# Sums of squares of four HGRN2 heads in quarters of the partitions, and first norm factors in the mixers' places, in a hybrid HGRN2 and Mamba-2 layer

## The chip, the cores and the metric

The kernel runs on one core of one Trainium2 chip. The metric is the device time of one execution in microseconds, and the number before the change is the median of three runs: 1939.81 us (1936.35 to 1941.0).

## The reference, cut to what matters

One layer on x of 2048 rows and 1024 columns. A projection of 6672 columns feeds 8 heads of an HGRN2 recurrence (128 keys, 128 values each) and 16 heads of Mamba-2 in two groups; both results are normed, concatenated to 2048 columns and projected back. The change touches the norm of each HGRN2 head, over its 128 values, and the place where its factor is applied:

```python
def hgrn2_mix(q_raw, f_raw, i_raw, g_raw, lb, norm_w):
    ...
    o = o.transpose(1, 0, 3, 2, 4).reshape(B_, L, HG_HEADS, HG_DV)
    o = o * lax.rsqrt(jnp.mean(o * o, axis=-1, keepdims=True) + EPS)
    o = o * norm_w.astype(jnp.float32).reshape(HG_HEADS, HG_DV)
    o = o.reshape(B_, L, HG_WIDTH) * jax.nn.silu(g_raw.astype(jnp.float32))
    return o.astype(q_raw.dtype)
def reference(x, norm_w, w_in, hg_lb_logits, hg_norm_w, m2_conv_w, m2_conv_b,
              m2_dt_bias, m2_a_log, m2_d_skip, m2_norm_w, w_out, final_norm_w):
    ...
        mix = jnp.concatenate([hg_out, m2_out], axis=-1)
        x = x + jnp.einsum('bse,ed->bsd', mix, w_out[l]).astype(x.dtype)
    return rmsnorm(x, final_norm_w)
```

## The kernel before, in words

**Tiling.** The 2048 rows are four blocks of TB = 512 (`tb`), each of NW = 4 windows of 128. Everything is kept transposed: features on the 128 partitions, rows along the free axis. A projection of 128 columns (`proj`, L344 to 354) is 24 matmuls of 128x512: weights and activations are each split into a high and a low part, and three products of 8 contraction steps are summed.

**Stages and their order.** The program is a list of jobs per block (`block_jobs`, L857 to 920): HGRN2 heads H(0) to H(7) (`hg_unit`, L608), four-part value projections VV (`v_step`), B and C of a Mamba-2 group (`bc_unit`), and eight units M of two Mamba-2 heads (`m2_unit`, L475). Each has projections, run one by one (`step`), and stages that are due a fixed count of projections later (`plan`, `flush`, L820 to 842). A head's stages m0 to m7 and mk are due 3 to 11 projections after its start (`DUES`), so the stages of neighbouring units stand between the projections of later ones. The Tile framework sets the semaphores; each engine works through its instructions in program order, and DMAs issued by SyncE (`nc.sync`) wait in SyncE's order too.

**The sums before.** Stage m6 of a head squares its output from PSUM into an "s" tile `on` (128x512) and stores the gated output to DRAM (`mix_d`). Stage m7 sums the squares over the partitions with `ss_cols` (L128): four matmuls, one per window, with the squares as weights and two columns of ones as the moving operand. VectorE copies the four column sums, GpSimd turns them into inverse roots with a power (`rstd_cols`, L120 to 123) in one column group of `nst`. At the block's end `rg_store` (L849) transposes `nst` (8 heads and 2 Mamba-2 groups, 40 rows) with TensorE, ScalarE copies it, and one DMA stores it to `rg_d[tb]`.

**Places in memory.** `slot` (L223) gives tiles of three tags in the mixers' pool `mp`: "s" (512 columns, 17 buffers), "b" (1024 columns, 8), "t3" (768, 2). The pool closes at `mid.close()` (L1018); pool `op` then uses its memory. Weights of the projection lie in `wp` with four buffers a tag (`wh`, `wl`, and three of `raw`) and are loaded PRE = 3 projections ahead (`w_get`, L112) through SyncE.

**Output projection** (L945 to 1071). Its blocks are the first three blocks and two halves of the last. `mix_get` (L961) loads a pair of normed-to-be rows e, e + 1 (`mr`), broadcasts their factors from `rg_d` to all partitions (`rgb`; for e < 8 one per head, L975), multiplies them in, and splits the result into `mh` and `ml`. `wo_get` (L947) loads one output weight and splits it (L952, L953). `out_mm` (L993) does three matmuls per output column group d. For block 0, five of eight column groups (`early`) of e = 0 to NE - 1 (NE = 8) are done in the last stages of the mixers, one `early_step` (L1010) a step; after `mid.close()` come e = NE to 15 for those five, then all 16 for the other three (`rest`). In the early steps the pairs e = 0 and 2 take the weights' `raw` buffers; the factors come from pool `o1`, with three buffers.

Of the kernel before, what the change touches and what calls it, by code (L numbers as in the profile page):

```python
# [7 lines left out]
F32 = mybir.dt.float32  # L8
# [30 lines left out]
def hybrid_layer(ctx, tc, xT, wt, wdt, wout, small, rows, out):  # L39
# [33 lines left out]
    rsk = rows[32:48].rearrange("(c h) -> h c", h=2)  # L73
    mhalf = cp.tile([P, 1], F32, name="mhalf")
    G.memset(mhalf, -0.5)
    epst = cp.tile([P, 1], F32, name="epst")
    G.memset(epst, EPS)

# [130 lines left out]
        V.tensor_add(sel, md32[0:32, 0:16], md32[0:32, 16:32])  # L209

    mix_d = [[dp.tile([P, TB], F32, name=f"mixd{e}_{t}") for t in range(NTB)] for e in range(16)]
    NR = (HG + 2) * NW
    rg_d = [dp.tile([NR, P], F32, name=f"rgd{t}") for t in range(NTB)]
    cs_d = [dp.tile([NW * M2H, P], F32, name=f"csd{t}") for t in range(NTB)]

    mid = ExitStack()
# [258 lines left out]
    def m2_unit(tb, g, c, ws, bcs, dts, sq, nst, r):  # L475
# [95 lines left out]
        def m3():  # L571
            ssv = ss_cols(sq["acc"], bank(f"mss{nm}"))
            ss = mp.tile([P, NW], F32, tag="mss", bufs=2, name=f"mss{nm}")
            V.tensor_copy(ss, ssv)
            rstd_cols(nst[:, HG + g, :], ss, 512)
        return [p0, p1], ([] if ct else [(1, ml)]) + list(zip(M0DUES if ct == 0 else MDUES, (md, m0, m1, m2))) + ([(9, m3)] if c == 3 else [])


# [26 lines left out]
                        A.copy(dst, ps)  # L605
        return [p0], []

    def hg_unit(tb, hd, ws, vrec, nst, r):  # L608
        nm = f"{hd}_{tb}"
        by32 = lambda a: a.rearrange("p (w t) -> p w t", t=32)  # L610

# [198 lines left out]
            advance(hgS[:, hd, :], NW - 1)  # L810

        def m7():
            ssv = ss_cols(r["on"], bank(f"hss{nm}"))
            ss = mp.tile([P, NW], F32, tag="hss", bufs=2, name=f"hss{nm}")
            V.tensor_copy(ss, ssv)
            rstd_cols(nst[:, hd, :], ss, P)
        return [pf, pq, pg], list(zip(DUES, (m0, m1, m2, m3, m4, mk, m5, m6, m7)))


# [28 lines left out]
    def rg_store(tb, nst):  # L848
        def m0():  # L849
            pt = bank(f"rgt{tb}")  # L850
            T.transpose(pt[0:NR, 0:P], nst.rearrange("p a w -> p (a w)"), ident)
            rgs = mp.tile([NR, P], F32, tag="cst", bufs=1, name=f"rgs{tb}")
            A.copy(rgs, pt[0:NR, 0:P])
            nc.sync.dma_start(rg_d[tb], rgs)
        return [], [(8, m0)]

    def block_jobs(tb):  # L857

        out_ = []
        dts, vrec, bcs, sq = {}, {}, {}, {}  # L860
        nst = mp.tile([P, HG + 2, NW], F32, tag="nst", bufs=2, name=f"nst{tb}")
        add = lambda fn, *args: out_.append((fn, args))

        def H(hd):
            add(hg_unit, tb, hd, [need(tb, c) for c in (8 + hd, hd, 24 + hd)], vrec.setdefault(hd // 4, {}), nst, {})

        def VV(q):
            ws = [need(tb, 16 + 4 * q + j) for j in range(4)]
            for j in range(4):
                add(v_step, tb, q, j, ws, vrec.setdefault(q, {}))  # L870

        def B(g):
            add(bc_unit, tb, g, [need(tb, 48 + g), need(tb, 50 + g)], bcs.setdefault(g, {}))

        def M(ct):
            add(m2_unit, tb, ct // 4, ct % 4, [need(tb, 40 + ct), need(tb, 32 + ct)], bcs.setdefault(ct // 4, {}),
                dts, sq.setdefault(ct // 4, {}), nst, {})

        def call(f):
            add(None, f)  # L880
        if tb == 0:
            H(0)
            VV(0)
            call(lambda: use(0))
        else:
            call(lambda: use(tb))
            VV(0)
        add(dt_unit, tb, dts)
        if tb:
            H(0)  # L890
        B(0)
        M(0)
        H(1)
        M(1)
        H(2)
        M(2)
        H(3)
        M(3)
        nxt = stats(tb + 1) if tb + 1 < NTB else [lambda: None] * 4
        call(nxt[0])  # L900
        VV(1)
        call(nxt[1])
        B(1)
        call(nxt[2])
        H(4)
        call(nxt[3])
        M(4)
        H(5)
        nxt = prep(tb + 1) if tb + 1 < NTB else [lambda: None] * 4
        M(5)  # L910
        call(nxt[0])
        H(6)
        call(nxt[1])
        M(6)
        call(nxt[2])
        H(7)
        call(nxt[3])
        M(7)
        add(rg_store, tb, nst)
        return out_  # L920
# [32 lines left out]
        V.tensor_sub(lo, raw, hi.bitcast(F32))  # L953
        wos[e] = (hi, lo)

    mixes, rgbs, xos = {}, {}, {}
    HB = TB // 2
    blocks = [(tb, 0, TB) for tb in range(NTB - 1)] + [(NTB - 1, 0, HB), (NTB - 1, HB, HB)]
    LAST = len(blocks) - 1
# [1 line left out]
    def mix_get(bl, e, lo=V):  # L961
# [8 lines left out]
            nc.sync.dma_start(mr[:, i, 0:n], mix_d[e + i][tb][:, cs_])  # L970
        if e < 8:
            for i in range(2):
                rgb = o1.tile([P, NW, P], F32, tag="rgb", bufs=3, name=f"rgh{bl}_{e}_{i}")[:, 0:n // P]
                r0 = (e + i) * NW + c0 // P
                nc.sync.dma_start(rgb, rg_d[tb][r0:r0 + n // P, :].partition_broadcast(P))  # L975
                V.tensor_tensor(mr[:, i, 0:n], mr[:, i, 0:n], rgb.rearrange("p w t -> p (w t)"), op=ALU.mult)
        else:
            if e in (8, 12):
                rgb = o1.tile([P, NW, P], F32, tag="rgb", bufs=3, name=f"rgb{bl}_{e}")[:, 0:n // P]
                r0 = (e // 4 + 6) * NW + c0 // P  # L980
                nc.sync.dma_start(rgb, rg_d[tb][r0:r0 + n // P, :].partition_broadcast(P))
                rgbs[bl, e // 4] = rgb.rearrange("p w t -> p (w t)")
# [20 lines left out]

    early = range(5)
    rest = range(5, KT)
    NE = 8
    o1 = ctx.enter_context(tc.tile_pool(name="o1", bufs=1))
    pss = {d: acc_bank(0, d) for d in early}

# [6 lines left out]
        step(lambda e=e: early_step(e))  # L1016
    flush(1 << 30)
    mid.close()  # L1018

    op = ctx.enter_context(tc.tile_pool(name="op", bufs=2))  # L1020
    accs, bks = {}, {}
# [110 lines left out]
```

## Time and profile before

| | |
|---|---|
| median of 3 runs (lowest, highest) | 1939.81 us (1936.35, 1941.0) |
| the profiled execution, its own time | 1938.97 us |
| its span in the trace | 1937.3 us |
| mean granted clock of TensorE | 0.990 |
| DVE (VectorE), share of the span | 62% |
| ACT (ScalarE), share of the span | 37% |
| POOL (GpSimd), share of the span | 17% |

PE is TensorE's matmuls, PEld its weight loads, which overlap them; SP is SyncE. Tile names stand without their numbers: `hss` is the sum of a head's squares, `on` the squares, `rgh` the factors of a pair e < 8, `woh` and `wol` the parts of an output weight, `po` the output projection's PSUM. A line such as L352 may be that of a helper that many stages call. In a timeline a row with a count is a run of like instructions, and its duration reaches from the first one's start to the last one's end. Matmuls are pipelined: one row's duration is longer than the distance to the next.

### The profile page before, as it was taken

Reading aid. Unit: us, or ns where it says so; the run is one execution under the profiler, and the core shown is the slowest. Engines: PE = TensorE matmul, PEld = TensorE weight load, DVE = VectorE, ACT = ScalarE, POOL = GpSimd, SP = SyncE. Lnnn points to the kernel's source line nnn. Section 1 sums busy time; section 2 is a strip of 40 time slices with the busy share of each in tenths; the row PEclk is TensorE's granted clock in tenths of the full one; section 3 lists DMA queues with packets and bytes.
Section 4 is the critical chain, followed back from the end, with each engine's and each line's share of the span. In section 5 each row is a group of like instructions: output and inputs, shape, how many; then the busy total and the mean of one; then the engine's idle time right before and its main releaser. Section 6 shows DMA issues by size and latency. Waiting matters only on the chain.

```text
span 1937.3 us, 34016 instructions
## 1 busy us (share of the span) xinstructions
PE 1895.2 (98%) x13418; PEld 1577.9 (81%) x13418; DVE 1203.2 (62%) x2920; ACT 710.3 (37%) x1170; POOL 323.2 (17%) x444
## 2 busy tenths in 40 slices
PE   7999999999999999999999999999999899999998
PEld 5788888788888888888888888888888777788897
DVE  8678768955565477547655874566366766534352
ACT  4446445533442353334333432334233433111111
POOL 4332242312011221110111211111101110000000
PEclk9999999999999999999999999999999899999998
DMA  8676876745555555455566554645455365524142
GB/s 267 246 261 240 285 256 227 267 153 176 178 172 195 177 194 185 150 172 180 163 207 189 194 173 143 194 156 167 169 186 164 133 240 177 201 82 152 47 134 88
DMA packets 118200, 355.44 MB, mean 183 GB/s; under 512 B 13032, under 2 KB 24472, under 8 KB 117656
## 3 DMA queue, kind: packets, MB, share of 16 engines
q1 hardware_dynamic: 116840, 352.00, 54.2%
q0 software_dynamic: 96, 0.03, 0.4%
q8 instruction: 106, 1.74, 0.4%
q10 hardware_dynamic: 1104, 1.24, 0.2%
q14 instruction: 54, 0.44, 0.1%
HBM read 273.30 MB, written 79.90 MB: 182 GB/s over the span
## 4 chain that ended last, share of the span: by engine, by line
PE 90%; DVE 5%; DMA 3%; ACT 1%; issue 1%; POOL 0%; ACTq 0%; DVEq 0%; SPq 0%; POOLq 0%
PE po L998 15%; PE px L352 9%; PE pz L352 9%; PE pf L352 9%; PE pv L597 9%; PE pq L352 9%; PE pg L352 8%; PE pB L352 2%; PE pC L352 2%; PE yd L546 2%; PE B L644 1%; PE o L804 1%; PE S L537 1%; PE hS L785 1%; PE o L803 1%; PE yo L557 1%
## 5 line engine op out<-in xcount | busy, mean ns | idle before, releaser
L998 PE MATMUL po<-mh,woh 128*128 128x512 f32 (+1 forms) x640 | 225.9, 355 | 9.7 <-ACT woh L952 9.7
L998 PE MATMUL po<-mh,wol 128*128 128x512 f32 (+1 forms) x640 | 224.3, 351 | 1.5 <-DVE wol L953 1.5
L998 PE MATMUL po<-ml,woh 128*128 128x512 f32 (+1 forms) x640 | 223.5, 351 | 2.0 <-DVE ml L989 2.0
L998 PEld LDWEIGHTS po<-mh,woh 128*128 128x128 f32 x640 | 122.3, 191 | 26.6 <-ACT woh L952 10.2
L998 PEld LDWEIGHTS po<-mh,wol 128*128 128x128 f32 x640 | 122.6, 192 | 19.3 <-DVE wol L953 3.4
L998 PEld LDWEIGHTS po<-ml,woh 128*128 128x128 f32 x640 | 122.1, 191 | 18.6 <-DVE ml L989 3.3
L988 ACT CAST mh<-mr 128x1024 fp32r<-128x1024 f32 (+1 forms) x48 | 43.4, 906 | 195.9 <-PE po L998 151.4
L989 DVE TENSOR_TENSOR ml<-mr,mh 128x1024 fp32r<-128x1024 f32 (+1 forms) x47 | 49.0, 1042 | 67.7 <-ACT mh L988 67.4
L510 DVE TENSOR_SCALAR csb<-csb,cs 128x128 f32<-128x128 f32 x256 | 66.7, 329 | 22.6 <-ACT ecs L507 22.6
L794 DVE SCALAR_TENSOR_TENSOR hSt<-hgS,totw,hS 128x128 f32<-128x128 f32 x32 | 11.0, 345 | 111.9 <-PE hS L785 99.2
L439 DVE SCALAR_TENSOR_TENSOR xs<-u_x,sm,xs 128x512 f32<-128x512 f32 x96 | 72.5, 755 | 4.2 <-ACT xs L437 3.7
L597 PE MATMUL pv<-wh,hh 128*128 128x512 f32 x224 | 72.0, 402 | 0.0
L569 POOL TENSOR_TENSOR sqa<-sqa,ecs 128x512 f32<-128x512 f32 x24 | 32.0, 1332 | 228.4 <-ACT ecs L568 191.9
L597 PE MATMUL pv<-wl,hh 128*128 128x512 f32 x224 | 69.5, 391 | 0.0
L597 PE MATMUL pv<-wh,hl 128*128 128x512 f32 x224 | 69.1, 390 | 0.0
L708 DVE TENSOR_TENSOR k<-k,tot 128x384 f32<-128x384 f32 x64 | 43.7, 683 | 40.8 <-PE B L644 40.8
L352 PE MATMUL px<-hh,wh 128*128 128x512 f32 x256 | 67.6, 406 | 0.0
L352 PE MATMUL pz<-hh,wh 128*128 128x512 f32 x256 | 67.6, 406 | 0.0
L352 PE MATMUL pq<-hh,wh 128*128 128x512 f32 x248 | 66.3, 410 | 0.0
L434 ACT COPY u_x<-px 128x512 f32<-128x512 f32 x32 | 18.8, 586 | 129.4 <-PE px L352 129.4
L352 PE MATMUL pf<-hh,wh 128*128 128x512 f32 x248 | 65.3, 405 | 0.0
L352 PE MATMUL pg<-hh,wh 128*128 128x512 f32 x248 | 65.0, 403 | 0.0
(333 smaller groups left out, 4597.8 us busy)
## 6 DMA issues: line engine op xcount, KB each, us to landing
wh<-whd SPq DMA_DIRECT2D x156, 512.0 KB, 4.3
wl<-wld SPq DMA_DIRECT2D x156, 512.0 KB, 3.4
whd<-wh SPq DMA_DIRECT2D x52, 512.0 KB, 3.4
wld<-wl SPq DMA_DIRECT2D x52, 512.0 KB, 3.0
wr<-wt SPq DMA_DIRECT2D x51, 512.0 KB, 5.3
csb<-csd SPq DMA_DIRECT2D x32, 512.0 KB, 5.5
mr<-mixd SPq DMA_DIRECT2D x64, 256.0 KB, 3.2
mixd<-sg SPq DMA_DIRECT2D x32, 256.0 KB, 2.0
```

Source lines behind the costliest of these rows:

```text
L352: state["mm"] = T.matmul(ps, lhsT=a[:, k, :], rhs=b[:, k, :], start=(n == 0), stop=(n == 23))
L439: V.scalar_tensor_tensor(dst, u[:, j:j + TB], cw[:, c, j:j + 1], dst, op0=ALU.mult, op1=ALU.add)
L510: V.tensor_scalar(csb[:, i, w, :], csb[:, i, w, :], dts["cs"][:, w, h0 + i:h0 + i + 1], 0.0, ALU.subtract, ALU.min)
L537: T.matmul(pS[:, sl], lhsT=bc["Bn"][:, w, :], rhs=xdc[:, sl], start=True, stop=True)
L546: T.matmul(pd[64 * i:64 * i + 64, w * P:(w + 1) * P], lhsT=xdt[:, w * P + i * 64:w * P + i * 64 + 64], rhs=csb[:, i, w, :], start=True, st ...
L557: T.matmul(po[:, sl], lhsT=prevs[w], rhs=bc["CT"][:, sl], start=True, stop=True)
L569: G.tensor_tensor(sq["acc"], sq["acc"], t, op=ALU.add)
L597: T.matmul(ps, lhsT=a[:, 2 * j + k, w * P:(w + 1) * P], rhs=rhs, start=(j == 0 and n == 0), stop=(j == 3 and n == 5))
L708: V.tensor_tensor(kv, kv, tt[:, :, 1:4].unsqueeze(3).broadcast_to([P, ng, 3, b]), op=ALU.mult)
L988: A.copy(mh[:, :, 0:n], mr[:, :, 0:n])
L989: lo.tensor_tensor(ml[:, :, 0:n], mr[:, :, 0:n], mh[:, :, 0:n].bitcast(F32), op=ALU.subtract)
L998: T.matmul(pss[d], lhsT=a[:, d, :], rhs=b, start=(e == 0 and n == 0), stop=(e == 15 and n == 2))
```

## The change

In m7 a head's squares go on a list `sqs` of its group of four heads, and nothing more is done until the fourth (heads 3 and 7). Then four matmuls with 32 columns of 1/128 as weights (`mean32`) and the four heads' squares as moving operands give the means of squares, each in its own 32 partitions of one PSUM tile. ScalarE copies the tile into the place of the fourth head's squares; SyncE stores one row of each quarter to `rg_d` (16 rows of 128), loads these 2048 values as 128 x 16, GpSimd takes mean + EPS to the power -1/2, and SyncE stores them back. `nst` and `rg_store` keep the two Mamba-2 groups only.

In the output projection's early steps the factors for e = 0 and 2 (four tiles) are taken from the "s" places while the mixers' pool is open; the `rgb` tag of `o1` has two buffers instead of three. NE is 9: one more early step, with seven output weights in `o1` and seven in `op`.

```diff
@@ -73,6 +73,8 @@
     rsk = rows[32:48].rearrange("(c h) -> h c", h=2)
     mhalf = cp.tile([P, 1], F32, name="mhalf")
     G.memset(mhalf, -0.5)
+    mean32 = cp.tile([P, 32], F32, name="mean32")
+    G.memset(mean32, 1.0 / P)
     epst = cp.tile([P, 1], F32, name="epst")
     G.memset(epst, EPS)
 
@@ -209,8 +211,8 @@
         V.tensor_add(sel, md32[0:32, 0:16], md32[0:32, 16:32])
 
     mix_d = [[dp.tile([P, TB], F32, name=f"mixd{e}_{t}") for t in range(NTB)] for e in range(16)]
-    NR = (HG + 2) * NW
-    rg_d = [dp.tile([NR, P], F32, name=f"rgd{t}") for t in range(NTB)]
+    NR = 2 * NW
+    rg_d = [dp.tile([(HG + 2) * NW, P], F32, name=f"rgd{t}") for t in range(NTB)]
     cs_d = [dp.tile([NW * M2H, P], F32, name=f"csd{t}") for t in range(NTB)]
 
     mid = ExitStack()
@@ -572,7 +574,7 @@
             ssv = ss_cols(sq["acc"], bank(f"mss{nm}"))
             ss = mp.tile([P, NW], F32, tag="mss", bufs=2, name=f"mss{nm}")
             V.tensor_copy(ss, ssv)
-            rstd_cols(nst[:, HG + g, :], ss, 512)
+            rstd_cols(nst[:, g, :], ss, 512)
         return [p0, p1], ([] if ct else [(1, ml)]) + list(zip(M0DUES if ct == 0 else MDUES, (md, m0, m1, m2))) + ([(9, m3)] if c == 3 else [])
 
 
@@ -605,7 +607,7 @@
                         A.copy(dst, ps)
         return [p0], []
 
-    def hg_unit(tb, hd, ws, vrec, nst, r):
+    def hg_unit(tb, hd, ws, vrec, sqs, r):
         nm = f"{hd}_{tb}"
         by32 = lambda a: a.rearrange("p (w t) -> p w t", t=32)
 
@@ -810,10 +812,22 @@
             advance(hgS[:, hd, :], NW - 1)
 
         def m7():
-            ssv = ss_cols(r["on"], bank(f"hss{nm}"))
-            ss = mp.tile([P, NW], F32, tag="hss", bufs=2, name=f"hss{nm}")
-            V.tensor_copy(ss, ssv)
-            rstd_cols(nst[:, hd, :], ss, P)
+
+            sqs.append(r["on"])
+            if len(sqs) < 4:
+                return
+            ps = bank(f"hss{nm}")
+            for j in range(4):
+                T.matmul(ps[32 * j:32 * j + 32, :], lhsT=mean32, rhs=sqs[j], start=True, stop=True)
+            rr = sqs[3]
+            A.copy(rr, ps)
+            flat = rg_d[tb][(hd - 3) * NW:(hd + 1) * NW, :].rearrange("w t -> (w t)")
+            nc.sync.dma_start(flat.rearrange("(j t) -> j t", j=4), rr.rearrange("(j r) t -> j r t", r=32)[:, 0, :])
+            rc = mp.tile([P, 16], F32, tag="rc", bufs=2, name=f"rc{nm}")
+            fold = flat.rearrange("(p c) -> p c", c=16)
+            nc.sync.dma_start(rc, fold)
+            rstd_cols(rc, rc, 1)
+            nc.sync.dma_start(fold, rc)
         return [pf, pq, pg], list(zip(DUES, (m0, m1, m2, m3, m4, mk, m5, m6, m7)))
 
 
@@ -851,18 +865,18 @@
             T.transpose(pt[0:NR, 0:P], nst.rearrange("p a w -> p (a w)"), ident)
             rgs = mp.tile([NR, P], F32, tag="cst", bufs=1, name=f"rgs{tb}")
             A.copy(rgs, pt[0:NR, 0:P])
-            nc.sync.dma_start(rg_d[tb], rgs)
+            nc.sync.dma_start(rg_d[tb][HG * NW:(HG + 2) * NW, :], rgs)
         return [], [(8, m0)]
 
     def block_jobs(tb):
 
         out_ = []
-        dts, vrec, bcs, sq = {}, {}, {}, {}
-        nst = mp.tile([P, HG + 2, NW], F32, tag="nst", bufs=2, name=f"nst{tb}")
+        dts, vrec, bcs, sq, hsq = {}, {}, {}, {}, {}
+        nst = mp.tile([P, 2, NW], F32, tag="nst", bufs=2, name=f"nst{tb}")
         add = lambda fn, *args: out_.append((fn, args))
 
         def H(hd):
-            add(hg_unit, tb, hd, [need(tb, c) for c in (8 + hd, hd, 24 + hd)], vrec.setdefault(hd // 4, {}), nst, {})
+            add(hg_unit, tb, hd, [need(tb, c) for c in (8 + hd, hd, 24 + hd)], vrec.setdefault(hd // 4, {}), hsq.setdefault(hd // 4, []), {})
 
         def VV(q):
             ws = [need(tb, 16 + 4 * q + j) for j in range(4)]
@@ -953,7 +967,7 @@
         V.tensor_sub(lo, raw, hi.bitcast(F32))
         wos[e] = (hi, lo)
 
-    mixes, rgbs, xos = {}, {}, {}
+    mixes, rgbs, xos, mixer_done = {}, {}, {}, []
     HB = TB // 2
     blocks = [(tb, 0, TB) for tb in range(NTB - 1)] + [(NTB - 1, 0, HB), (NTB - 1, HB, HB)]
     LAST = len(blocks) - 1
@@ -970,13 +984,15 @@
             nc.sync.dma_start(mr[:, i, 0:n], mix_d[e + i][tb][:, cs_])
         if e < 8:
             for i in range(2):
-                rgb = o1.tile([P, NW, P], F32, tag="rgb", bufs=3, name=f"rgh{bl}_{e}_{i}")[:, 0:n // P]
+                nm = f"rgh{bl}_{e}_{i}"
+                rgb = slot("s", [NW, P], nm) if e < 4 and not mixer_done else o1.tile(
+                    [P, NW, P], F32, tag="rgb", bufs=2, name=nm)[:, 0:n // P]
                 r0 = (e + i) * NW + c0 // P
                 nc.sync.dma_start(rgb, rg_d[tb][r0:r0 + n // P, :].partition_broadcast(P))
                 V.tensor_tensor(mr[:, i, 0:n], mr[:, i, 0:n], rgb.rearrange("p w t -> p (w t)"), op=ALU.mult)
         else:
             if e in (8, 12):
-                rgb = o1.tile([P, NW, P], F32, tag="rgb", bufs=3, name=f"rgb{bl}_{e}")[:, 0:n // P]
+                rgb = o1.tile([P, NW, P], F32, tag="rgb", bufs=2, name=f"rgb{bl}_{e}")[:, 0:n // P]
                 r0 = (e // 4 + 6) * NW + c0 // P
                 nc.sync.dma_start(rgb, rg_d[tb][r0:r0 + n // P, :].partition_broadcast(P))
                 rgbs[bl, e // 4] = rgb.rearrange("p w t -> p (w t)")
@@ -1003,7 +1019,7 @@
 
     early = range(5)
     rest = range(5, KT)
-    NE = 8
+    NE = 9
     o1 = ctx.enter_context(tc.tile_pool(name="o1", bufs=1))
     pss = {d: acc_bank(0, d) for d in early}
 
@@ -1016,6 +1032,7 @@
         step(lambda e=e: early_step(e))
     flush(1 << 30)
     mid.close()
+    mixer_done.append(True)
 
     op = ctx.enter_context(tc.tile_pool(name="op", bufs=2))
     accs, bks = {}, {}
```

## Rows read from the trace of the kernel before

**Rows 1.** The page's chain that ended last: its shares by engine.
```profile
PE 90%; DVE 5%; DMA 3%; ACT 1%; issue 1%; POOL 0%; ACTq 0%; DVEq 0%; SPq 0%; POOLq 0%
```

**Rows 2.** Windows: start:end, us, busy (count) of each engine, PE clock, DMA, GB/s.
```profile
60.00:1526.00 1466.00, 1463.01 (x11026) 1211.76 (x11025) 936.65 (x2486) 586.14 (x992) 278.77 (x398) 1.00 0.58 191
345.00:385.00 40.00, 37.01 (x304) 30.77 (x303) 36.59 (x78) 19.27 (x33) 14.16 (x14) 0.96 0.77 283
1531.00:1549.00 18.00, 10.97 (x78) 8.66 (x77) 15.72 (x32) 9.60 (x12) 4.18 (x5) 0.72 0.77 258
1580.00:1601.00 21.00, 16.96 (x61) 12.68 (x59) 9.76 (x10) 7.23 (x8) 1.54 (x1) 0.84 0.60 223
```

**Rows 3.** PE's waits: for what, us in total, times, longest.
```profile
PE po L998 <- ACT woh L952: 9.7, 2, 6.0
```

**Rows 4.** Timeline of PE around two sums: start, duration, line, operation.
```profile
1502.60 0.95 PE L129 MATMUL hss<-ones,on 128*128 128x2 f32 x8
1503.47 0.33 PE L738 MATMUL H<-qa,k 128*32 128x32 f32 x16
...
1507.49 1.98 PE L352 MATMUL pq<-hl,wh 128*128 128x512 f32 x8
1509.40 0.45 PE L760 MATMUL G<-qa,k 128*64 128x64 f32 x8
...
1573.95 0.39 PE L998 MATMUL po<-ml,woh 128*128 128x512 f32 x1
1574.18 0.95 PE L129 MATMUL hss<-ones,on 128*128 128x2 f32 x8
1574.98 0.49 PE L998 MATMUL po<-mh,woh 128*128 128x512 f32 x1
1575.31 0.40 PE L998 MATMUL po<-mh,wol 128*128 128x512 f32 x1
```

**Rows 5.** PE: timeline at hb and B; line 149 (min/median/max ns); group of B.
```profile
324.74 1.02 PE L149 MATMUL hb<-dg_h,ones 128*128 128x512 f32 x2
...
L149 PE MATMUL hb<-dg_h,ones x6: 591/592/595, 324.7 to 1086.9; 128*128 128x512 f32 x6
...
1525.26 0.55 PE L644 MATMUL B<-MB,k 128*32 128x48 f32 x32
1525.74 0.50 PE L352 MATMUL pz<-hh,wh 128*128 128x512 f32 x1
...
L644 PE MATMUL B<-MB,k 128*32 128x48 f32 x2048 | 35.4, 210 | 3.9 <-DVE MB L681 3.9
```

**Rows 6.** Line 123: count, ns min/median/max, first to last start, form.
```profile
L123 POOL TENSOR_TENSOR rsx<-rsx,mhalf x4: 1008/1025/1852, 28.4 to 1033.8; 128x4 f32<-128x4 f32 x4
L123 POOL TENSOR_TENSOR orz<-orz,mhalf x1: 697/697/697, 1927.7 to 1927.7; 128x2 f32<-128x2 f32 x1
```

**Rows 7.** DMA issues: queue, count, KB each, median us to landing.
```profile
csd<-cst SPq DMA_DIRECT2D x4, 32.0 KB, 2.1
...
rgh<-rgd SPq DMA_DIRECT2D x32, 256.0 KB, 3.6
```

**Rows 8.** Timeline of SyncE's queue: start, us to issue, line, transfer.
```profile
1502.79 0.32 SPq L102 DMA_DIRECT2D wh<-whd  x1
...
1531.53 1.27 SPq L975 DMA_DIRECT2D rgh<-rgd  x3
```

**Rows 9.** Timeline at qa, dg_h, xdc; line 699 with its first and last start.
```profile
1084.95 0.28 ACT L699 COPY qa<-MB 128x128 f32<-128x128 f32 x1
1085.06 1.03 DVE L148 TENSOR_SCALAR dg_h<-ident,rsx 128x128 f32<-128x128 f32 x4
...
L699 ACT COPY qa<-MB x32: 283/289/300, 45.9 to 1533.8; 128x128 f32<-128x128 f32 x32
...
1555.12 0.69 DVE L523 TENSOR_TENSOR xdc<-xn,dec 128x512 f32<-128x512 f32 x1 [0.19 <-ACT xn L521]
```

**Rows 10.** The chain that ended last, 1580 to 1600 us, in order.
```profile
1584.14 1.31 DMA rgd<-rgs
```

## The prediction, made before the changed kernel ran

> **What bounds the kernel now.** I read the page's chain first: TensorE is 90% of the work that ended last [rows 1], VectorE the next with 5%. The windows then say where this is true. From 60 to 1526 us PE is busy 1463.01 of 1466 us at the granted clock 1.00, so there each microsecond of PE work is a microsecond of time [rows 2]. Three other stretches lose time [rows 2]. From 345 to 385, the end of the first block, PE is busy 37.01 of 40 us and VectorE, on which it then waits, 36.59. From 1531 to 1549, where the output projection begins, PE is busy 10.97 of 18 us at a granted clock of 0.72; by the waits of PE its longest one there (6.0) is for the first output weight's cast [rows 3]. From 1580 to 1601, where the mixers' memory is given back, it is busy 16.96 of 21 us at 0.84, and the other of the two waits in rows 3 (9.7 in all) stands there. The profiled execution took 1938.97 us, 1.67 more than its span and 0.84 less than the median of the runs; the sum is made against 1938.97. A measurement of this kernel tells about 0.3%, 5.8 us, from no change.
>
> **Sums removed.** Each of 32 heads has four matmuls with two moving columns, eight passes [rows 4]. The passes are short, but each loads 128 columns of weights first. Before wide matmuls: from the last wide start at 1573.95 to the second after the sums, 1575.31, is 1.36 us; two steps of a stream take 0.46 (eight wide passes take 1.98, the last alone 0.39, so one step is 0.23). The sums cost 0.90 [rows 4]. Before a group that uses quarters of the array: they hold PE from 1502.60 to 1503.47, 0.87. Without them such a group starts 0.32 after the last wide start (1509.40 against 1507.49 + 1.98 - 0.39 = 1509.08), 0.09 over a step, so they cost 0.78 [rows 4]. The first head of the kernel and every fourth one stand before wide work, nine in all: 9 x 0.90 + 23 x 0.78 = 26.0 us.
>
> **Sums added.** Eight times, four matmuls of 32 weight columns over 512 columns of f32, two passes each. The nearest pass of this length and type is the broadcast of the row factors: two take 1.02, one 0.59, so a step is 0.43 [rows 5]. Whether four go beside each other is read from the group B: 32 passes of 48 columns into the four quarters. One after another they would take 32 x 0.43 x 48/512 = 1.29; they take 0.55 less the last one's 0.21, 0.34, nearly a quarter [rows 5]. So two steps, 0.86. Changing shape costs 0.09 going in and 0.10 coming out (the next wide start is 0.14 after B's last, which streams 0.04), and the second wide start comes 0.33 instead of 0.23 later [rows 4, 5]. That is 1.15 each, 9.2 in all. Bounds: 6.9 without changes of shape; 8 x (8 x 0.43 + 0.29) = 29.8 if none overlap. I take 9.2, since B has the same shape and only fewer columns. Net -16.8.
>
> The Trainium skill, "TensorE: Matmul & The Clock Gate", section "Measured speedup vs the span model", gives less for 512 columns: 3.07 times for four row tiles, 2.38 for three column tiles. By 3.07 the two steps would be 1.12 and the whole result 2 us later; no run here shows it yet, and B's rows speak for nearly four.
>
> **Off the path.** VectorE loses 32 copies of four columns, ScalarE gains eight copies of 512 columns (128 take 0.28 [rows 9], so between that and 1.1; I take 0.6), and the transposition of the factors shrinks from 40 to 8 rows: nothing, as PE work hides them. GpSimd's power on 16 columns isn't in the trace: two columns take 0.70, four 1.02 [rows 6], so 0.16 a column gives 2.9 us; bounds 1.0 and 4.1. SyncE issues three small transfers in a row for each four heads: store, load, store, each waiting for what the one before it brings. A small store lands in 2.1, a broadcast load in 3.6 [rows 7], so the chain is 0.6 + 2.1 + (2.1 to 3.6) + 3.1 + 2.1, 10 to 11.5 us. GpSimd stands in it too, with the convolutions' products and the att copies behind it. On SyncE the next weights and csb loads stand behind it; the weights of the last pz were asked for at 1502.79 and used at 1525.74 [rows 5, 8], 23 us ahead, about 18 after landing. So a chain is hidden seven times of eight, up to a length of 18 us; beyond it, every microsecond counts. The last one isn't hidden (below).
>
> **First block.** By its end PE would come some 3.6 us earlier (a quarter of 16.8, less what is still to come), but VectorE gives back only eight short copies and is full. I take 3 us of the 16.8 as lost there, between 0 and 5.
>
> **First norm factors.** Before, SyncE stood still for the projection memory and asked for the first three factor loads together at 1531.53 [rows 8], when the last projection had ended. The edit puts the four of e = 0 and 2 in "s" slots, but places with one tag seem to be handed out in program order: the broadcast dg_h needs only rsx, whose last power began at 1033.8 [rows 6], yet it was written at 1085.06, just after the "s" tile that precedes it in the program, qa at 1084.95 [rows 9]. The last "s" tile ahead of the first factors is qa of the last head, written at 1533.81, later than 1531.53. So they are asked for about 2.3 us later, behind the loads for e = 4 and 6, which still go into the freed memory: a loss of 1 to 5, I take 2.5. The factors of e = 2 stand in the program behind the last xdc, which was written at 1555.12 [rows 9], about when PE came to e = 2; if its place is older than that the load costs nothing, else some 6, I take 2. Together +4.5. If the order does not bind, the loads land before 1531 and the 7.03 us in which PE idles from 1531 to 1549 go, and a share of 10.97 us at lowered clock, some 10 in all, of which VectorE (15.72 busy of 18 [rows 2]) lets about 8 through.
>
> **One more early step, and the give-back.** The mixers' memory now waits for the last chain instead of the factor store, which landed at 1584.14 + 1.31 = 1585.45 [rows 10], 11.3 after the last head's sums began at 1574.18 [rows 4]. The new chain ends 11 to 12.6 after them. But PE has 15 more matmuls, 3.45 us, before it needs that memory. What then ends last is the weight load that needs the freed memory for its cast, shifted alike. So 3.45 less 0 to 1.3: -2, with bounds -6 and +2.
>
> **Two buffers for factors instead of three.** In the second pass over block 0 each pair would wait for a load (3.6) and two products (0.69 each, as xdc in rows 9), 5.0 us, where PE uses a pair in 18 x 0.23 = 4.1; only four pairs come so and mixes run up to four ahead. +1, between 0 and 4. The later blocks use a pair in 11 us, or 5.7 with half the columns: nothing.
>
> **Sum:** -16.8 + 3 + 4.5 - 2 + 1 = -10.3, so 1928.7.
>
> **The rivals.**
> Early factors (0.17): the places are free and the loads go ahead, so the gap at 1531 closes. For it: SyncE had nothing else to do for 28 us; against it: the order in rows 9. The place then gives -8 instead of +4.5: 1916.
> Sums one after another (0.10, slower): at 512 columns the four streams do not overlap, or a head's second pass holds back the next head's first. Place: PE, eight times; price 29.8 instead of 9.2. It decides from 3.0 us a group on, where the removal is used up. Then +3.8 + 4.5 - 2 + 1, and no lead for the first block to take: 1946. Against it stands B.
> Held squares (0.13): three more of 17 "s" slots are held for up to a hundred microseconds, so a drain of PSUM takes a slot just read and waits for a lagging engine; with two projection banks PE feels it once the wait passes a projection (24 wide steps, 5.5 us). At 0.3 us a head 10 us go: 1938. Against it: nothing yet waits so in steady state.
> Chains too long (0.10): SyncE or GpSimd stand longer than 18 us in some of the eight chains; 4 us each for four of them: 1944. Against it: the landings.
>
> **How the numbers follow.** The forecast has 0.50, 1928.7; its own range is 1921 to 1936. To hold 8 in 10 the range reaches down through the early factors and up through held squares to the lower part of the slow cases: 1912 to 1944. Faster by over 0.3%: 0.47 of the forecast, all 0.17, 0.04 of the others, 0.68. Within: 0.20, most of it held squares and chains. Slower: 0.12, from the serial sums and long chains.
>
> **What would show it.** Eight groups hss of 8 passes, about 1.1 us of PE each (1 right, 3.7 serial); windows from 60 to 340 and 400 to 1500 shorter by 2 and 10 us with PE full; PE waits near 345 to 385 longer than 3 us; the factor loads of e = 0 after 1533 in the old time, and the first wait of the output projection 6 to 9 us; at the give-back a wait for a cast of e = 9 under 3.6. PE waiting for a weight or for an "s" tile in the middle of a block would make the sum wrong, as would factor loads well ahead of the last projection.

## The result, and the profile after

The changed kernel takes 1922.87 us (median of 4 runs, 1920.79 to 1926.49), the kernel before 1939.46 in the same comparison; the ratio is 0.9918 (95% interval 0.9899 to 0.9938). That is 16.6 us less where 10.3 were forecast: inside the range, and larger than forecast. The profiled execution took 1923.20 us with a span of 1921.3, so the pair of profiles differs by 15.8 us.

The windows of the changed kernel, columns as in [rows 2]; the four stretches are the ones shown of before, moved with the work:

```profile
60.00:1512.00 1452.00, 1448.25 (x10845) 1182.95 (x10844) 934.68 (x2460) 589.81 (x1000) 262.07 (x354) 1.00 0.58 194
345.00:385.00 40.00, 36.25 (x296) 29.63 (x295) 37.08 (x76) 19.57 (x33) 14.53 (x12) 0.96 0.80 291
1517.00:1535.00 18.00, 9.83 (x90) 7.59 (x88) 14.88 (x31) 8.47 (x12) 3.63 (x5) 0.72 0.68 222
1566.00:1587.00 21.00, 19.20 (x88) 15.10 (x87) 8.76 (x10) 5.49 (x7) 7.31 (x6) 1.00 0.58 213
```

TensorE is as full and at full clock in the blocks as before, only shorter. The start of the output projection is no better (9.83 us busy of 18 at a granted clock of 0.72, against 10.97 [rows 2]); the give-back is much better (19.20 of 21 at 1.00, against 16.96 at 0.84).

The timeline of PE in the changed kernel: the last projection, the first matmul of the output projection, that of its third step (e = 2), and the last group of sums:

```profile
1511.83 0.50 PE L354 MATMUL pz<-hh,wh 128*128 128x512 f32 x1
...
1528.75 0.79 PE L1014 MATMUL po<-mh,woh 128*128 128x512 f32 x1 [8.01 <-ACT woh L966]
...
1547.76 0.50 PE L1014 MATMUL po<-mh,woh 128*128 128x512 f32 x1 [0.53 <-ACT mh L1004]
...
1563.98 0.39 PE L1014 MATMUL po<-ml,woh 128*128 128x512 f32 x1
1564.30 1.07 PE L821 MATMUL hss<-on,mean 128*32 128x512 f32 x8
1565.29 0.50 PE L1014 MATMUL po<-mh,woh 128*128 128x512 f32 x1
1565.63 0.39 PE L1014 MATMUL po<-mh,wol 128*128 128x512 f32 x1
```

and the groups of the two new operations, the sums and GpSimd's power on 16 columns:

```profile
L821 PE MATMUL hss<-on,mean 128*32 128x512 f32 x64 | 8.5, 605 | 0.0
...
L125 POOL TENSOR_TENSOR rc<-rc,mhalf 128x16 f32<-128x16 f32 x8 | 23.3, 2912 | 0.7
```

The sums cost TensorE what was worked out: from the wide start at 1563.98 to the second one after them, 1565.63, are 1.65 us, less two steps of 0.23 leaves 1.19 (forecast 1.15). Eight passes of 605 ns lie in 1.07 us.

To see where the time went, the starts of the same matmul are compared: the first head of the second block (`pf`), the last projection (`pz`), and then, counted from the last projection, the first matmul of the output projection, that of its third and of its eighth step; the way from the eighth step to the twelfth, with the give-back in it; from there to block 1; the first 96 matmuls of block 1; and the rest to the end. All are read from the timelines of PE, one profile each (the experiments' labels are told below):

| kernel | 2nd block | last pz | first | 3rd step | 8th step | give-back | to block 1 | block 1 | rest |
|---|---|---|---|---|---|---|---|---|---|
| before | 435.87 | 1525.74 | 14.96 | 28.48 | 53.60 | 20.92 | 51.25 | 24.71 | 261.05 |
| changed | 433.68 | 1511.83 | 16.92 | 35.93 | 58.13 | 16.02 | 50.51 | 22.63 | 262.13 |
| e1 sums only | 431.76 | 1509.93 | 14.96 | 27.17 | 55.10 | 22.02 | 51.44 | 23.05 | 261.18 |
| e2 places only | 437.92 | 1527.78 | 17.17 | 37.57 | 59.75 | 19.67 | 51.31 | 24.19 | 261.34 |
| e3 nine steps only | 439.19 | 1529.12 | 14.96 | 29.01 | 56.90 | 16.13 | 51.29 | 22.67 | 261.03 |
| e4 no places | 434.24 | 1512.39 | 14.96 | 26.94 | 53.43 | 15.68 | 51.59 | 22.63 | 261.77 |
| e5 early request | 434.24 | 1512.41 | 8.83 | 17.15 | 43.70 | 18.51 | 50.24 | 23.68 | 261.11 |
| e6 ACT's queue | 435.95 | 1514.12 | 17.75 | 39.05 | 63.24 | 16.07 | 50.53 | 22.63 | 261.15 |
| e7 = e4, small tiles outside | 435.23 | 1512.66 | 14.96 | 27.24 | 53.67 | 13.88 | 51.31 | 23.21 | 261.06 |
| e8 = e1, small tiles outside | 432.82 | 1510.25 | 14.97 | 27.28 | 55.29 | 13.90 | 51.51 | 23.71 | 262.02 |
| e9 = e5, small tiles outside | 431.15 | 1508.59 | 8.84 | 17.16 | 45.22 | 15.46 | 49.89 | 22.63 | 261.06 |
| e10 serial sums | 435.65 | 1529.14 | 16.92 | 37.15 | 62.98 | 15.15 | 51.07 | 22.63 | 261.66 |
| e11 sums twice | 433.95 | 1517.46 | 17.51 | 37.06 | 61.22 | 15.46 | 50.91 | 22.63 | 261.14 |
| e12 early request only | 440.25 | 1530.09 | 8.84 | 18.04 | 44.92 | 20.15 | 51.03 | 23.67 | 261.06 |

Of the 16.0 us between the two spans, 13.9 are there by the last projection. The tail then loses 4.5 up to the eighth step and wins 4.9 at the give-back, 0.7 before block 1 and 2.1 at its start; the end takes 1.1 back. The chain that ended last shows the two places, the first factors and the give-back (start, duration, work):

```profile
1519.14 0.24 PE o L806 x2
1519.43 5.25 DMA rgh<-rgd
1524.70 1.27 DVE mr L992
...
1565.35 2.41 POOL ml L1005
1567.77 2.52 DMA mr<-mixd
...
1572.96 2.90 POOL rc L125
1575.88 0.32 SPq L830
...
1576.30 1.22 DMA rgd<-rgs
...
1577.84 1.05 ACT woh L966
1578.89 0.04 issue
1578.94 21.08 PE po L1014 x91
```

The first two rows: the load of the first factors could only start (1519.43) when the matmuls `o` of the last head but one had read the place it was given (1519.14 + 0.24). The last rows: GpSimd's power, the store of the factors, behind it in SyncE's queue the store of the Mamba-2 rows (1576.30), and only when that has landed the casts into freed memory.

### The profile page after: what moved, and what is told of

The parts are those of the page before. It is cut to its first block, busy times and chain, and to the rows that moved or that the text cites. A ratio compares the mean times of both kernels' runs of the same rounds, so it can differ in the third digit from the quotient of the medians.

```text
span 1921.3 us, 33571 instructions
## 1 busy us (share of the span) xinstructions
PE 1877.7 (98%) x13226; PEld 1546.0 (80%) x13226; DVE 1197.7 (62%) x2887; ACT 713.3 (37%) x1178; POOL 306.2 (16%) x398
## 4 chain that ended last, share of the span: by engine, by line
PE 92%; DVE 4%; DMA 2%; issue 1%; ACT 1%; POOL 0%; DVEq 0%; ACTq 0%; SPq 0%; POOLq 0%
PE po L1014 18%; PE px L354 9%; PE pz L354 9%; PE pf L354 9%; PE pv L599 9%; PE pq L354 9%; PE pg L354 8%; PE pB L354 2%; PE pC L354 2%; PE yd L548 2%; PE B L646 2%; PE o L806 1%; PE o L805 1%; PE S L539 1%; PE yo L559 1%; PE hS L787 1%
## 5 line engine op out<-in xcount | busy, mean ns | idle before, releaser
L1014 PE MATMUL po<-mh,woh 128*128 128x512 f32 (+1 forms) x640 | 223.0, 352 | 10.3 <-ACT woh L966 9.8
L1014 PEld LDWEIGHTS po<-mh,woh 128*128 128x128 f32 x640 | 121.5, 190 | 28.2 <-ACT woh L966 10.3
L1014 PEld LDWEIGHTS po<-mh,wol 128*128 128x128 f32 x640 | 121.6, 190 | 16.8 <-DVE wol L967 1.1
L438 POOL COPY hist<-u_x 128x3 f32<-128x3 f32 x32 | 9.7, 304 | 395.7 <-ACT u_x L436 395.6
L436 ACT COPY u_x<-px 128x512 f32<-128x512 f32 x32 | 18.8, 587 | 128.7 <-PE px L354 128.7
```

Source lines behind the costliest of these rows:

```text
L1014: T.matmul(pss[d], lhsT=a[:, d, :], rhs=b, start=(e == 0 and n == 0), stop=(e == 15 and n == 2))
```

## The experiments

**The change taken apart.** Four kernels make each edit alone or leave one out. The sums alone (e1) have `NE = 8` and these factor tiles:

```diff
-rgb = slot("s", [NW, P], nm) if e < 4 and not mixer_done else o1.tile(
-    [P, NW, P], F32, tag="rgb", bufs=2, name=nm)[:, 0:n // P]
+rgb = o1.tile([P, NW, P], F32, tag="rgb", bufs=3, name=nm)[:, 0:n // P]
```

> Only the sums of four heads in quarters; first factors from the projection memory, three factor buffers and eight early steps, as before. Theory A, three separate parts: the sums give 13.9 us up to the last projection and take 0.6 back at the last group; at the give-back of the mixers' memory the longer chain (13.2 us from sums to store, 11.3 before) costs 2 more; the wait of 1.7 us in the second pass over block 0 stays. 1939.5 - 13.9 + 0.6 + 2 = 1928. Theory B, the tail gains by the sums too, because GpSimd and VectorE have less to do at the end, and the other two edits do nothing: 1923.

Measured: 1925.28 us (0.9926 of before, 0.9911 to 0.9941), between the two theories. The sums alone bring most of the gain. The give-back is 1.1 us longer than before (22.02), the longer chain; but the tail as a whole is only 1.3 us longer, as the third step (27.17) and the start of block 1 (23.05) come sooner. So part of the tail's gain does come with the sums, and neither theory holds fully.

The places alone (e2) are put into the kernel before, with three buffers and `NE = 8`:

```diff
-rgb = o1.tile([P, NW, P], F32, tag="rgb", bufs=3, name=f"rgh{bl}_{e}_{i}")[:, 0:n // P]
+rgb = slot("s", [NW, P], nm) if e < 4 and not mixer_done else o1.tile(
+    [P, NW, P], F32, tag="rgb", bufs=3, name=nm)[:, 0:n // P]
```

> Only the first factors in the mixers' places, with the sums, the eight early steps and three factor buffers of before. Theory A: no difference up to the last projection, first matmul of the output projection about 2 us later, third step (e = 2) later by up to 8, some 4 left by e = 4: 1943. Theory B: the places do nothing or help a little: 1936 to 1940.

Measured: 1946.47 us, ratio 1.0026 (1.0014 to 1.0038): slower, and by the table where theory A puts it: first matmul 2.21 us later, third step 9.09. The step of the change that was meant to feed the first matmuls delays them.

The ninth step alone (e3), also in the kernel before:

```diff
-NE = 8
+NE = 9
-tag="rgb", bufs=3
+tag="rgb", bufs=2
```

> Only nine early steps and two factor buffers; sums as before, first factors from the projection memory. Theory A: 5.7 us less at the give-back and 2.0 less in the second pass over block 0: 1932. Theory B: with two buffers the factor loads of the early steps wait for each other and the ninth step gives nothing: 1938 to 1942.

Measured: 1939.91 us, 0.9992 (0.9983 to 1.0002): by the total nothing, in theory B's range, and theory A's 1932 is ruled out. By the table the give-back is 4.8 us shorter and the first matmuls of block 1 take 2.0 less, as theory A has it, but the eighth step comes 3.3 us later, where PE now waits for the Mamba-2 squares, which it did not before:

```profile
PE mss L129 <- POOL sqa L569: 2.0, 1, 2.0
```

In this profile the tail is 3.5 us shorter, and 5.6 us were lost at the end of the first block, where the instructions are those of before. The mechanism of theory A is seen; the gain that it forecast is not.

The change without the places (e4) has the factors in `o1` with `bufs=2` and `NE = 9`:

```diff
-rgb = slot("s", [NW, P], nm) if e < 4 and not mixer_done else o1.tile(
-    [P, NW, P], F32, tag="rgb", bufs=2, name=nm)[:, 0:n // P]
+rgb = o1.tile([P, NW, P], F32, tag="rgb", bufs=2, name=nm)[:, 0:n // P]
```

> The changed kernel with the first factors taken from the projection memory (two buffers) in place of the mixers' places. Theory A: the 3.9 us that the places cost by e = 4 come back: 1919. Theory B: with two buffers for the four pairs of the early steps their loads queue up, and the places are what lets nine steps go: 1926 to 1930.

Measured: 1917.97 us (0.9888, 0.9868 to 0.9909), 4.9 us below the change. The two intervals overlap, but the table has the difference where theory A puts it: the third step 9.0 us sooner, the eighth 4.7, the tail as a whole 4.3. Two buffers are enough for the early steps.

The three single edits change the medians by -15.4, +5.8 and -0.7 us, -10.3 together, where the whole change gave -16.6. The ninth step with two buffers is worth 7.3 us behind the new sums (from e1 to e4) and next to nothing in the kernel before (e3). So one edit's worth depends on the others by these medians; the intervals are too wide to rule out that the parts add up.

**Why the first factors come late.** SyncE's timeline in the changed kernel:

```profile
1517.61 0.80 SPq L984 DMA_DIRECT2D mr<-mixd  x2
1518.46 1.77 SPq L991 DMA_DIRECT2D rgh<-rgd  x3
...
1539.15 0.33 SPq L963 DMA_DIRECT2D wor<-wout  x1
1539.53 0.90 SPq L991 DMA_DIRECT2D rgh<-rgd  x2
...
1567.77 0.32 SPq L984 DMA_DIRECT2D mr<-mixd  x1
1568.18 0.51 SPq L825 DMA_DIRECT2D rgd<-on  x1
```

and two rows of ScalarE and VectorE near these loads:

```profile
1519.89 0.29 ACT L701 COPY qa<-MB 128x128 f32<-128x128 f32 x1
...
1540.46 0.69 DVE L525 TENSOR_TENSOR xdc<-xn,dec 128x512 f32<-128x512 f32 x1
```

SyncE stood before the load of e = 4 until the projection memory came free (1517.61). The factors of e = 0 were behind it and then waited for their own place, which came free some 0.5 us after SyncE had got to them; those of e = 2 were issued at 1539.53, right behind an output weight that had waited for its buffer. Two experiments part the place from the queue. In e5 the four rows go into two places of the "b" tag, of which the last block uses fewer, and are asked for behind M(5), ten projections from the end:

```diff
+        M(5)
+        if tb == NTB - 1:
+            call(load_firsts)
...
+    def load_firsts():
+        for e in (0, 2):
+            firsts[e] = slot("b", [2, NW, P], f"rgf{e}")
+            for i in range(2):
+                nc.sync.dma_start(firsts[e][:, i], rg_d[0][(e + i) * NW:(e + i + 1) * NW, :].partition_broadcast(P))
...
+rgb = firsts[e][:, i] if e < 4 and not mixer_done else o1.tile(
+    [P, NW, P], F32, tag="rgb", bufs=2, name=nm)[:, 0:n // P]
```

> The changed kernel, but the first four factor rows go into two of the mixers' larger places (the tag of 1024 columns), taken and loaded some six projections before the last one. Theory A, the 's' places come free only when the last head but one has been read, after the last projection: with places that are free earlier e = 0 and e = 2 come in time, the 1.96 and the 8.3 us go, and the idle time before the first matmul of the output projection shrinks too: 1909 to 1917. Theory B, the first matmul is set by the casts of the weights and by VectorE anyway: as with the factors in the projection memory, 1918. Theory C, SyncE's queue gets longer before the last projections and late weights cost more: above 1923.

Measured: 1910.46 us (0.9844, 0.9827 to 0.9861). The first output matmul comes 8.83 us after the last projection began instead of 16.92, the third step 18.8 us sooner. The loads went out 83 and 76 us before the last projection began, and the products of e = 0 began at 1434.28, so part of VectorE's work left the start of the output projection as well. The windows of the two stretches show the first stall nearly gone, with the clock at 1.00, though VectorE is busy 17.05 of 18 us; at the give-back, which comes some 13 us earlier in this kernel, PE still idles 2.8 us for a cast:

```profile
1518.00:1536.00 18.00, 17.88 (x143) 14.47 (x142) 17.05 (x36) 13.27 (x22) 2.94 (x5) 1.00 0.64 212
1556.00:1577.00 21.00, 18.22 (x75) 14.58 (x75) 8.85 (x10) 5.61 (x7) 4.32 (x4) 0.92 0.70 262
...
1429.54 0.86 SPq L877 DMA_DIRECT2D rgf<-rgd  x2
...
PE po L1025 <- ACT woh L976: 2.8, 1, 2.8
```

In e6 the four loads stay in the "s" places but ScalarE issues them:

```diff
-nc.sync.dma_start(rgb, rg_d[tb][r0:r0 + n // P, :].partition_broadcast(P))
+(nc.scalar if e < 4 and not mixer_done else nc.sync).dma_start(
+    rgb, rg_d[tb][r0:r0 + n // P, :].partition_broadcast(P))
```

> The changed kernel with the four first factor loads issued by ScalarE instead of SyncE. Theory A, the place of e = 0 is late by itself and the loads of e = 2 are late by SyncE's queue: first matmul still about 2 us later than before against the last projection, the third step some 6 us earlier than in the changed kernel. Theory B, both are late by SyncE's queue: both as before the change or better, 1919. Theory C, ScalarE's casts stand behind the loads' waits and everything is later: above 1925.

Measured: 1929.47 us in one run, in the range of theory C, and as it has it everything is later (first matmul 17.75, third step 39.05). ScalarE's queue:

```profile
1521.71 0.84 ACTq L991 DMA_DIRECT2D rgh<-rgd  x2
...
1542.53 0.53 ACT L773 COPY att<-G 64x128 f32<-64x128 f32 x2 [1.59 <-PE G L762]
...
1543.11 0.81 ACTq L991 DMA_DIRECT2D rgh<-rgd  x2
```

The first load starts at 1521.71, 7.59 us after the last projection began, as in the changed kernel (1519.43 - 1511.83 = 7.60): the place, not the queue, sets e = 0. For e = 2 theory A missed: ScalarE asked for those factors at 1543.11, 29.0 after the last projection began, 1.3 us later than SyncE had (27.7), behind copies that waited for TensorE. So e = 2 is late in either queue, by what stands ahead of it there.

**The give-back.** The pool's memory comes back as a whole, so its last reader counts. In e7 and e8 the small tiles at the end of the last chain lie in the constants' pool; e7 is e4 with it, e8 is e1:

```diff
-rc = mp.tile([P, 16], F32, tag="rc", bufs=2, name=f"rc{nm}")
+rc = cp.tile([P, 16], F32, tag="rc", bufs=2, name=f"rc{nm}")
...
-rgs = mp.tile([NR, P], F32, tag="cst", bufs=1, name=f"rgs{tb}")
+rgs = cp.tile([NR, P], F32, tag="rgs", bufs=1, name=f"rgs{tb}")
...
-nst = mp.tile([P, 2, NW], F32, tag="nst", bufs=2, name=f"nst{tb}")
+nst = cp.tile([P, 2, NW], F32, tag="nst", bufs=2, name=f"nst{tb}")
...
-ss = mp.tile([P, NW], F32, tag="mss", bufs=2, name=f"mss{nm}")
+ss = cp.tile([P, NW], F32, tag="mss", bufs=2, name=f"mss{nm}")
```

> The kernel without the mixers' places for factors (two buffers, nine early steps), and the last chain's small tiles (the 128 x 16 factors, the transposed rows, the Mamba-2 sums) in the constants' pool, so that the mixers' memory waits only for the store of the copied sums, some 8 us earlier. Theory A, the give-back waits for the chain: the wait for the cast at the give-back goes, 1 to 2 us less than without this edit: 1916 to 1917. Theory B, the casts there wait for VectorE or for a weight's transfer: 1918.

> Only the sums of four heads (eight early steps, three buffers), with the last chain's small tiles in the constants' pool. Theory A: the give-back wait, which was 2.6 us longer with the longer chain, becomes shorter than in the kernel before, and the ninth early step is not needed: 1925.3 - 5 to 7 = 1918 to 1920. Theory B, the ninth step is what counts, because the first weight after the give-back is 10 us away in any case: 1924 to 1926.

Measured: 1915.08 (e7; 0.9863, 0.9840 to 0.9887) and 1917.51 (e8; 0.9878, 0.9864 to 0.9893): 2.9 us below e4 (the intervals overlap) and 7.8 below e1 (they don't). In both the give-back takes 13.9 us; 60 matmuls at 0.227 take 13.6. So the stall there was the wait for the chain and what followed from it, and with the chain out of the way the ninth step is not needed for it: e8 has eight.

Both edits together (e9 is e5 with the small tiles outside):

> Both edits that helped: first factors asked for early in the mixers' larger places, and the last chain's small tiles in the constants' pool. Theory A, they work on different waits (the first matmuls of the output projection; the give-back): the wait for a cast of 2.8 us at the give-back of the early kernel goes and 2 to 3 us are won on it: 1907 to 1909. Theory B, once the first matmuls come 12 us earlier the give-back waits for weights from DRAM and casts: 1910.

Measured: 1907.86 us (1904.84 to 1909.29; 0.9845, 0.9828 to 0.9861), the lowest median of all and 15 us below the change; its ratio and e5's are alike, so the totals don't tell the two apart. The table does: the give-back takes 15.46 us instead of 18.51, while the eighth step comes 1.5 later (45.22 instead of 43.70). The chain that ended last in e5, with the store and then the casts and a weight load in it, and in e9, where TensorE goes through the same stretch without waiting for memory:

```profile
1560.21 2.91 POOL rc L125
...
1563.55 1.22 DMA rgd<-rgs
...
1565.02 1.05 ACT woh L976
...
1567.35 9.22 DMA wor<-wout
```

```profile
1548.43 2.74 POOL ml L1016
1551.17 1.68 POOL sqa L571
...
1552.89 1.05 PE mss L131 x8
1553.95 5.15 PE po L1025 x15
1559.10 0.11 PE rgt L865
1559.21 25.86 PE po L1025 x114
```

What is left in e9 there is a wait for GpSimd (1.99 us, before the eighth step), which makes `ml` of a late pair before the Mamba-2 squares, and behind it a stretch at a lowered clock, in which PE is never idle:

```profile
1556.00:1560.00 4.00, 4.00 (x14) 3.06 (x14) 3.67 (x4) 1.80 (x4) 1.30 (x2) 0.67 0.92 316
```

The early request alone, in the kernel before (e12):

> The kernel before with one edit: the first four factor rows asked for early, in two of the mixers' larger places (sums, eight early steps and three buffers as before). Theory A: the first matmuls of the output projection come 6 and then 12 us earlier against the last projection, and half or more of it survives the give-back, where the longer wait takes some back: 1928 to 1934. Theory B: without the ninth step the give-back waits for the chain and takes all of it back: 1938 to 1941.

Measured: 1934.95 us (0.9968, 0.9955 to 0.9982), just outside theory A's 1934. By the table it keeps 10.7 us of the tail; this profile lost more than others ahead of the second block (440.25).

**The price of the sums.** In e10 all four sums of a group go into one set of 32 partitions as one accumulation, so that no head gets a factor of its own; in e11 each group is done twice:

```diff
-T.matmul(ps[32 * j:32 * j + 32, :], lhsT=mean32, rhs=sqs[j], start=True, stop=True)
+T.matmul(ps[0:32, :], lhsT=mean32, rhs=sqs[j], start=(j == 0), stop=(j == 3))
...
-A.copy(rr, ps)
+A.copy(rr[0:32], ps[0:32])
```

```diff
 for j in range(4):
     T.matmul(ps[32 * j:32 * j + 32, :], lhsT=mean32, rhs=sqs[j], start=True, stop=True)
+for j in range(4):
+    T.matmul(ps[32 * j:32 * j + 32, :], lhsT=mean32, rhs=sqs[j], start=True, stop=True)
```

> The changed kernel, but the four sums of a group go into the same 32 partitions, one after another as one accumulation (so the four heads get one common sum, and the output differs). Theory A, the four streams of the changed kernel run beside each other: here six steps of 0.43 more in each of eight groups, 2.6 each, 20.7 in all, of which the last group's may partly be waited away: 1940 to 1944. Theory B, they did not overlap much: 1923 to 1930.

> The changed kernel with each group's four sums done twice into the same partitions. Theory A: a second group without a change of shape costs two steps, 0.87, in each of eight: 6.9 more, 1930. Theory B, there is time on TensorE that costs nothing: 1923 to 1925.

Measured, one run each: 1944.67 and 1930.67 us. The group row of e10, whose passes take 29.0 us where the changed kernel's take 8.5, and its last group in the timeline:

```profile
L821 PE MATMUL hss<-on,mean 128*32 128x512 f32 x64 | 29.0, 595 | 0.0
...
1584.22 3.62 PE L821 MATMUL hss<-on,mean 128*32 128x512 f32 x8
```

Between the second block and the last projection, with six groups, e10 takes 15.3 us more than the changed kernel, 2.56 a group, and e11 5.4, 0.89 a group. So four sums in four quarters cost two steps of 0.43 where one quarter costs eight. "TensorE: Matmul & The Clock Gate" of the Trainium skill, section "Measured speedup vs the span model", gives 2.38 times for three column tiles of 32 at 512 columns, 0.79 a tile. This case's trace, which has four such tiles, shows more a tile: by the distance of the starts they took 0.434 + 0.43 us where eight passes one after another take 8 x 0.43, 3.98 times; from the first start to the end of the last row, 1.07 against 3.62 us, 3.4 times. The measurement decides. Without the overlap the gain is gone: e10 takes 1944.67 us, the kernel before 1940.69 (1936.32 to 1947.08) in the same comparison.

## Why the prediction was right, and where it was not

**Sums: right.** Removed and added sums were forecast at -16.8, a fourth of it a block. In the changed kernel the second block starts 2.19 us sooner, the third 6.37, the fourth 10.56: 4.18 a block. At each place a removed sum shows as 0.79 (the first 0.81) and a new group as 0.28 more than the sum it replaces. The landmarks show no loss from the held squares or from the seven hidden chains: from the second block to the last projection nothing moved but these steps. Those two rivals fall, and with e10 the third, whose break-even should read 26.0 / 8 = 3.25 us a group and not 3.0.

**First block: too large.** 3 us were taken as lost at its end. The second block starts 2.19 us sooner, 2.3 less than the 4.46 that the sums up to there are worth (six removed, one replaced by a group). But 1.50 of this was lost before the first sum, as the first projection of Mamba-2 shows, which stands ahead of all sums (before, then changed):

```profile
88.55 0.71 PE L352 MATMUL px<-hh,wh 128*128 128x512 f32 x2
...
90.05 0.71 PE L354 MATMUL px<-hh,wh 128*128 128x512 f32 x2
```

From this matmul to the second block are 347.32 us before and 343.63 in the changed kernel, so 0.8 us was lost. In the eight profiles with the new sums (e10 and e11 apart) it is 342.96 to 345.52, 0.1 to 2.7 lost, 1.2 on average. Two kernels with the old sums took 352.90 (e3) and 351.10 (e12), with the instructions of before up to there, so the stretch varies by more than the term. That the 13.9 us by the last projection agree with the 13.8 forecast, which counts the last group too, is partly luck: 1.5 of what is missing is of the start, for which the sum had no term.

**First factors: right in size, wrong in cause.** +4.5 forecast; the eighth step is 4.53 later, and e4 without them 4.9 faster. Two signs named ahead came: the load of e = 0 at 1533.3 in the old time, and a first wait of 8.01 us. The parts agree less: e = 0 cost 2.0 us at the first matmul, e = 2 another 5.5 at the third step where 2 were taken, and 2.9 came back by the eighth, which is luck. But places were not handed out in the order of the program: the load began at 1519.43, before `qa` of the last head was written at 1519.89; it waited for the matmuls that read the place before. And the load of e = 2 came before the last `xdc` (1539.53 against 1540.46): what held it was a weight ahead of it in the queue. The early-factors rival was right about what the stall is worth (-8 to the eighth step; e5 has 43.70 against 53.60, -9.9) and wrong that this edit would bring it.

**Give-back: the wait as forecast, the clock behind it left out.** -2 was forecast, -4.9 measured. The wait for the cast went from 3.64 to 1.75 us, 1.9 less, as forecast. The rest is the clock behind the wait, for which the sum had no term (before, then changed; each wait and the window behind it):

```profile
1586.80 1.22 PE L998 MATMUL po<-mh,woh 128*128 128x512 f32 x2 [3.64 <-ACT woh L952]
...
1586.80:1593.00 6.20, 6.16 (x14) 4.42 (x15) 4.80 (x5) 1.84 (x2) 0.00 (x0) 0.50 0.98 374
...
1578.94 1.45 PE L1014 MATMUL po<-mh,woh 128*128 128x512 f32 x5 [1.75 <-ACT woh L966]
...
1579.00:1586.00 7.00, 7.00 (x31) 5.61 (x32) 5.87 (x6) 2.85 (x3) 0.00 (x0) 1.00 1.01 397
```

Before, 14 matmuls behind the wait took 6.20 us at a granted clock of 0.50, its lower level of 1.2 GHz; 14 steps of 0.227 are 3.2, so 3.0 us went there. In the changed kernel the clock stayed at 1.00. A second size was off: the chain took 13.2 us from the sums (1564.30) to the landing (1576.30 + 1.22), not 11 to 12.6, in part since its first store (1568.18) stood in SyncE's queue behind a load (1567.77) that waited for GpSimd's `ml` (1565.35 + 2.41).

**Two buffers: no cost seen.** +1 was forecast. From the twelfth step to block 1 it takes 51.25 us before and 51.29 and 51.59 in the kernels with two buffers and no places (e3, e4). That it takes 50.51 in the changed kernel isn't shown to come of the buffers. No term foresaw the 2.1 us at block 1's start, where before PE waited 1.7 us for `ml`. There e1, which has three buffers, is 1.7 shorter too, so it does not take two buffers for that. What does it stays open.

## What to carry to other kernels

A place that is free "earlier" helps a load only if the place's last reader and the loads ahead in the queue are done earlier too: ask when both are, not where the tile lies. When a pool is given back as a whole, its memory waits for the last small tile of the longest chain; a few hundred bytes a partition in another pool were worth 2.6 to 7.8 us by the medians (only the 7.8 of e8 is clear of noise), as much as another step of work to hide the wait: e8 takes 1917.51 us with eight steps, e4 1917.97 with nine. When a wait is priced, look at the granted clock behind it too: here the clock gave back 3.0 us and the wait 1.9. The sums of four heads in four quarters cost 1.19 us, one head's sum as eight passes of two columns 0.79 to 0.90.

## What the runs showed of the hardware that was not expected

Four f32 matmuls of 128x32 weights over 512 columns start within 20 ns of each other and the next four 0.434 us later: full overlap, where the group B of [rows 5] had shown nearly that at 48 columns. Issued by ScalarE, a load that is wanted early came 1.3 us later (one run) than by a SyncE that had stood still for 27 us. Behind a wait of 3.64 us the clock was at its lower level for 6.2 us, behind one of 1.75 it was not, and behind one of 1.99 (e9) eight matmuls again started some 0.43 us apart instead of 0.23. And the second block began up to 4.8 us apart in the eight profiles with the new sums, whose instructions up to there are the same or nearly so, more than most terms of the sum; up to 3.0 of it is there before the first sum.
